# Gate and up projections of four SwiGLU layers as seven products of half width, two chunks at a time

## The chip, the cores and the metric

The kernel runs on one core of a Trainium2 chip. The metric is the device time of one execution in microseconds; for the kernel before it is the median of three runs. The engines of a core are TensorE (PE; PEld is its loading of stationary blocks), VectorE (DVE), ScalarE (ACT), GpSimd (POOL) and SyncE (SP, which here only issues transfers). Each executes its own instructions in order and waits on the others by semaphores.

## What is computed

A trunk of two decoder layers on 512 tokens of width 1024, in float32. Each layer is: half a SwiGLU feed-forward, a token mixer, half a SwiGLU feed-forward, a gated embedding. The mixer is a gated linear recurrence (HGRN) in the first layer and latent attention (MLA) in the second. The change touches the feed-forward layers:

```python
def _rmsnorm(x, g):
    y = x * lax.rsqrt(jnp.mean(x * x, axis=-1, keepdims=True) + EPS)
    return y * g

def _swiglu(h, w_in, w_out):            # w_in: 1024 x 5632, w_out: 2816 x 1024
    gate, up = jnp.split(h @ w_in, 2, axis=-1)
    return (jax.nn.silu(gate) * up) @ w_out

for li in range(2):
    x = x + 0.5 * _swiglu(_rmsnorm(x, g[0]), ffn_w_in[li, 0], ffn_w_out[li, 0])
    h = _rmsnorm(x, g[1])
    x = x + mixer(h)                    # HGRN for li = 0, MLA for li = 1
    x = x + 0.5 * _swiglu(_rmsnorm(x, g[2]), ffn_w_in[li, 1], ffn_w_out[li, 1])
    x = x + sigmoid(_rmsnorm(x, g[3]) @ ple_w_gate[li]) * (p[li] @ ple_w_in[li])
return _rmsnorm(x, final_norm)
```

## The kernel before

Features lie on the 128 partitions and the 512 tokens on the free axis, so x is eight tiles of 128x512. A float32 product is made of three matmuls: each operand is split into a rounded half `hi` and the rest `lo`, and `mm3` (L141) adds hi·hi, hi·lo and lo·hi in PSUM.

All weights lie in one stream in HBM, `wall`, in the order of their use, in tiles of eight blocks of 128x128 (512 KB). `block` (L129) hands out the blocks; at the start of a tile it calls `fetch` (L115): SP loads the tile into one of three `raw` buffers (L119), ACT casts it to one of three `whi` buffers (L125), DVE subtracts to one of three `wlo` buffers (L126). `chain` (L147) runs the three matmuls for every block of the contraction and leaves a PSUM bank.

`ffn` (L233) is called four times. It runs two halves of 11 chunks of 128 hidden features. A chunk takes one tile for its gate chain and one for its up chain, 24 matmuls of 128x512 each. `rb` is the reciprocal root mean square of each token, spread over the partitions; the operand `xg` (split x times gain) doesn't hold it, so both chains are multiplied by it afterwards: DVE times rb (L240), ACT silu (L241), POOL times rb (L242), DVE up times gate (L243), and a split (L157 on ACT, L158 on DVE). After the 11 chunks come eight output chains over the 11 hidden tiles, and DVE adds half of each to x (L249). In the second half `post(m)` prepares the next stage's operand for each x tile as it is done, and `beside` puts unrelated small work in (rotary tables, an embedding).

What sets the order: the program is written for one core, and a scheduler orders each engine's instructions, by the order of the code and by priorities (`soon` draws a fetch or an eviction ahead). Within an engine the order is then fixed. Slots come from rings: `slot` takes the next buffer of a tag (s, v, r, o, p, b), and an instruction that writes a slot waits for the last reader of its former content. PSUM has two rings of four banks, `mm` and `aux`.

In the trace the stages follow each other: start to 33 us, first FFN to 381, HGRN to about 663, second FFN to 1042, embedding and shared keys to 1150, third FFN to 1480, MLA to 1800, fourth FFN to 2150, the last embedding and norm to 2222.

Of the kernel before, what the change touches and what calls it, by code (L numbers as in the profile page):

```python
# [9 lines left out]
F32 = mybir.dt.float32  # L10
F32R = mybir.dt.float32r
I32 = mybir.dt.int32
AF = mybir.ActivationFunctionType
# [9 lines left out]
NF = DFF // P  # L23
NH = NF // 2
A_HEADS = 8
# [29 lines left out]
def kernel(  # L55
# [38 lines left out]

    BUFS = {"s": 38, "v": 9, "r": 14, "o": 8, "p": 6, "b": 4}
    FETCH_OFF = 200
# [17 lines left out]

    def fetch(pieces=1):  # L115
        i = stream["tiles"]
        stream["tiles"] += 1
        raw = wpool.tile([P, WB * P], F32, tag="raw", bufs=3, name=name("raw"))
        nc.sync.dma_start(raw, wall[i])  # L119
        hi = wpool.tile([P, WB * P], F32R, tag="whi", bufs=3, name=name("whi"))  # L120
        lo = wpool.tile([P, WB * P], F32R, tag="wlo", bufs=3, name=name("wlo"))
        n = WB * P // pieces
        for p in range(pieces):
            s = slice(p * n, (p + 1) * n)
            act.copy(hi[:, s], raw[:, s])  # L125
            dve.tensor_tensor(out=lo[:, s], in0=raw[:, s], in1=hi[:, s].bitcast(F32), op=ALU.subtract)  # L126
        stream["ready"].append((hi, lo))

# [103 lines left out]

    def ffn(xg, rb, post, beside=None, primed=()):  # L233
        primed = list(primed)
        for half in range(2):
            hidden = []
            for f in range(NH):
                pg, pu = (primed.pop(0) if primed else chain(xg) for _ in range(2))
                g = slot("g", F32, "r")
                dve.tensor_tensor(out=g, in0=pg, in1=rb, op=ALU.mult)  # L240
                act.activation(g, g, AF.Silu)  # L241
                pool.tensor_tensor(out=g, in0=g, in1=rb, op=ALU.mult)  # L242
                dve.tensor_tensor(out=g, in0=pu, in1=g, op=ALU.mult)  # L243
                hidden.append(split(g, None, "o" if f < 4 else "v" if f < 8 else "s"))
                if half == 1 and f == 5 and beside is not None:
                    beside()
# [433 lines left out]
    def shared(sh, sin, cos):  # L680
        st, lat, kr = sh.st, sh.lat, sh.kr
        tab = slot("tab")
        pool.tensor_scalar(out=tab[0:64, :], in0=cos[0:64, :], scalar1=1.0, scalar2=1.0, op0=ALU.mult, op1=ALU.mult)
        pool.tensor_scalar(
            out=tab[64:128, :], in0=sin[64:128, :], scalar1=cs[64:128, C_SIGN : C_SIGN + 1], scalar2=1.0,
            op0=ALU.mult, op1=ALU.mult,
        )
        kt = slot("kt")
        dve.tensor_tensor(out=kt, in0=kr, in1=tab, op=ALU.mult)
        pj = aux_bank()  # L690
        pe.matmul(pj, jmat, kt, start=True, stop=True)
        krope = split(pj)
        _, rc = rows(st)
        cn = []
        for m in range(2):
            c = slot("cn")
            dve.scalar_tensor_tensor(
                out=c, in0=lat[m], scalar=gain(V_LAT, m), in1=rc, op0=ALU.mult, op1=ALU.mult
            )
            cn.append(split(c))  # L700
        return cn, krope


    def mla(xg, stats, cn, krope, sin, cos, post):
# [13 lines left out]
        def rope(group):  # L718
            pa, pb = chain(cq), chain(cq)
            qa, qb, ta, tb = (slot("rt", F32, "p") for _ in range(4))  # L720
            act.copy(qa, pa)
# [3 lines left out]
            dve.tensor_tensor(out=ta, in0=ta, in1=tb, op=ALU.subtract)  # L725
            h1, l1 = split(ta, None, "b")
# [3 lines left out]
            h2, l2 = split(qb, None, "b")  # L730
            res = []
# [164 lines left out]

    ffn(first.xg[0], rb, n1, prepare, primed)
# [4 lines left out]
    ffn(n2.xg[0], rows(n2.stats)[1], n3, lambda: held.append(embed(0)))  # L902
    n4 = Next([gcol(1, 0)])
# [14 lines left out]
    n5 = Next([gcol(1, 1)])  # L918
    ffn(n4.xg[0], rb, n5)
    n6 = Next([gcol(1, 2)])  # L920
    mla(n5.xg[0], n5.stats, cn, krope, sin, cos, n6)
    n7 = Next([gcol(1, 3)])
    ffn(n6.xg[0], rows(n6.stats)[1], n7, lambda: held.append(embed(1)))
    last(n7.xg[0], held[1], rows(n7.stats)[1])
# [12 lines left out]
def _stream(i):  # L937
    out = []

    def ffn(l, n):  # L940
        wi = i["ffn_w_in"][l, n]
        wo = i["ffn_w_out"][l, n]
        for half in range(2):
            for f in range(half * NH, half * NH + NH):
                out.append(_blocks(wi[:, f * P : (f + 1) * P]))
                out.append(_blocks(wi[:, DFF + f * P : DFF + (f + 1) * P]))
            out.append(_blocks(wo[half * NH * P : (half + 1) * NH * P]))

# [137 lines left out]
```

## Time and profile before

| | us |
|---|---|
| median of 3 runs (2223.89 to 2224.09) | 2224.09 |
| the profiled execution | 2224.34 |
| its span in the profile | 2222.2 |
| PE busy | 2200.4 |
| DVE busy | 1158.4 |
| ACT busy | 774.4 |
| POOL busy | 423.3 |

The span runs from the first to the last instruction of the profiled execution; the rest of its time lies around it. A busy share is a mean over stages; the windows of a stage show which engine it waits for. In rows of the timeline the first number is the start, the second the duration; in grouped rows stand the count, the busy time, the mean of one in ns and the idle time before them with what ended it.

### The profile page before, as it was taken

The page shows a single profiled execution, that of the slowest core. Times are in us where ns is not written, and L with a number is a line of the kernel's source. Part 1 is how long each engine was busy: PE and PEld are TensorE (multiplying, and loading weights), DVE is VectorE, ACT ScalarE, POOL GpSimd, SP SyncE. Part 2 cuts the span into 40 slices and gives each one's busy share as a digit, 9 for nine tenths or more (in the row PEclk, how much of TensorE's full clock was granted, in tenths as well). Part 3 has the DMA queues.
Part 4 walks back from the last instruction along what each step waited for, and adds up shares of the span by engine and source line. Part 5 has one row for each costly group of instructions (what it writes and reads, how often), then busy time and mean ns, then how long its engine had stood idle before and what let it go on. Part 6 is the DMA issues. An engine that isn't in the chain of part 4 may idle for free.

```text
span 2222.2 us, 26413 instructions
## 1 busy us (share of the span) xinstructions
PE 2200.4 (99%) x10434; PEld 1845.4 (83%) x10434; DVE 1158.4 (52%) x1798; ACT 774.4 (35%) x1125; POOL 423.3 (19%) x441
## 2 busy tenths in 40 slices
PE   8999999999999999999999999999999999999998
PEld 6888888899888888888888888888888888888887
DVE  5333544778775433444654333457677764334445
ACT  4222333323333322334533222346444443223244
POOL 2100111454522100111121011112111121001111
PEclk9999999999999999999999999999999999999999
DMA  4332332222223233333232333323223122333332
GB/s 161 102 96 95 100 95 93 87 61 67 67 67 105 95 95 96 109 99 95 86 105 95 95 97 101 97 86 96 66 85 92 53 86 95 95 95 108 101 95 67
DMA packets 60523, 204.42 MB, mean 92 GB/s; under 512 B 7408, under 2 KB 9584, under 8 KB 60400
## 3 DMA queue, kind: packets, MB, share of 16 engines
q1 hardware_dynamic: 59536, 201.28, 28.9%
q8 instruction: 82, 1.34, 0.3%
q10 hardware_dynamic: 864, 1.46, 0.2%
q14 instruction: 41, 0.34, 0.0%
HBM read 196.42 MB, written 2.10 MB: 89 GB/s over the span
## 4 chain that ended last, share of the span: by engine, by line
PE 96%; DVE 2%; ACT 1%; issue 0%; DMA 0%; POOL 0%; SPq 0%; DVEq 0%; ACTq 0%
PE mm L142 29%; PE mm L143 29%; PE mm L144 29%; PE aux L396 1%; PE aux L143 1%; PE aux L144 1%; PE aux L142 1%; PE aux L800 1%; PE aux L774 0%; PE aux L775 0%; PE aux L205 0%; PE aux L213 0%; DVE wlo L126 0%; PE aux L196 0%; DVE lo L158 0%
## 5 line engine op out<-in xcount | busy, mean ns | idle before, releaser
L143 PE MATMUL mm<-lo,whi 128*128 128x512 f32 x2824 | 1103.1, 391 | 2.1 <-DVE lo L161 2.0
L142 PE MATMUL mm<-hi,whi 128*128 128x512 f32 x2824 | 1095.8, 391 | 8.8 <-ACT whi L125 6.4
L144 PE MATMUL mm<-hi,wlo 128*128 128x512 f32 x2824 | 1100.7, 390 | 0.0
L125 ACT CAST whi<-raw 128x1024 fp32r<-128x1024 f32 (+2 forms) x372 | 386.4, 1041 | 1096.6 <-PE mm L143 790.8
L142 PEld LDWEIGHTS mm<-hi,whi 128*128 128x128 f32 x2824 | 530.5, 188 | 118.0 <-ACT whi L125 6.4
L143 PEld LDWEIGHTS mm<-lo,whi 128*128 128x128 f32 x2824 | 530.9, 188 | 110.9 <-DVE lo L161 4.1
L144 PEld LDWEIGHTS mm<-hi,wlo 128*128 128x128 f32 x2824 | 530.8, 188 | 108.5 <-DVE wlo L126 0.7
L126 DVE TENSOR_TENSOR wlo<-raw,whi 128x1024 fp32r<-128x1024 f32 (+2 forms) x372 | 463.6, 1248 | 271.3 <-ACT whi L125 251.4
L242 POOL TENSOR_TENSOR g<-g,rb 128x512 f32<-128x512 f32 x88 | 152.3, 1733 | 984.0 <-ACT g L241 984.0
L243 DVE TENSOR_TENSOR g<-mm,g 128x512 f32<-128x512 f32 x88 | 60.8, 691 | 263.5 <-PE mm L144 255.0
L240 DVE TENSOR_TENSOR g<-mm,rb 128x512 f32<-128x512 f32 x88 | 60.4, 690 | 206.0 <-PE mm L144 206.0
L179 POOL TENSOR_TENSOR sq<-sq,sq 128x512 f32<-128x512 f32 x55 | 80.5, 1464 | 335.2 <-ACT sq L174 334.3
L249 DVE SCALAR_TENSOR_TENSOR x<-mm,x 128x512 f32<-128x512 f32 x64 | 44.2, 690 | 106.8 <-PE mm L144 105.6
L160 ACT ACTIVATE hi<-x,vc 128x512 fp32r<-128x512 f32 x72 | 51.4, 718 | 77.1 <-DVE x L249 57.3
L789 POOL TENSOR_SCALAR P<-P,t 128x128 f32<-128x128 f32 (+1 forms) x64 | 35.3, 551 | 220.3 <-DVE t L788 189.1
L161 DVE SCALAR_TENSOR_TENSOR lo<-x,vc,hi 128x512 fp32r<-128x512 f32 x72 | 63.0, 883 | 25.2 <-ACT hi L160 25.1
L158 DVE TENSOR_TENSOR lo<-g,hi 128x512 fp32r<-128x512 f32 x88 | 60.0, 684 | 0.9 <-ACT hi L157 0.7
L786 ACT ACTIVATE P<-P,t,t 128x128 f32<-128x128 f32 (+1 forms) x64 | 42.0, 656 | 47.0 <-DVE t L783 46.8
L157 ACT CAST hi<-g 128x512 fp32r<-128x512 f32 x88 | 54.5, 621 | 6.9 <-DVE g L243 6.9
L241 ACT ACTIVATE g<-g 128x512 f32<-128x512 f32 x88 | 55.0, 628 | 1.4 <-DVE g L240 1.2
L142 PE MATMUL mm<-whi,hi 128*128 128x256 f32 x192 | 55.2, 288 | 0.0
L143 PE MATMUL mm<-wlo,hi 128*128 128x256 f32 x192 | 55.0, 287 | 0.0
(199 smaller groups left out, 1576.0 us busy)
## 6 DMA issues: line engine op xcount, KB each, us to landing
raw<-in_wall SPq DMA_DIRECT2D x367, 512.0 KB, 3.5
x<-in_xT SPq DMA_DIRECT2D x8, 256.0 KB, 6.3
qr<-hi SPq DMA_DIRECT2D x32, 64.0 KB, 2.0
qr<-lo SPq DMA_DIRECT2D x32, 64.0 KB, 2.0
out_dram<-o SPq DMA_DIRECT2D x8, 256.0 KB, 2.5
p<-in_pT ACTq DMA_DIRECT2D x4, 256.0 KB, 2.7
cs<-in_cst SPq DMA_DIRECT2D x1, 385.0 KB, 7.4
pos<-in_pos ACTq DMA_DIRECT2D x1, 256.0 KB, 3.3
```

What stands on the lines that cost most here:

```text
L125: act.copy(hi[:, s], raw[:, s])
L126: dve.tensor_tensor(out=lo[:, s], in0=raw[:, s], in1=hi[:, s].bitcast(F32), op=ALU.subtract)
L142: pe.matmul(out, a[0], b[0], start=first, stop=False)
L143: pe.matmul(out, a[0], b[1], start=False, stop=False)
L144: pe.matmul(out, a[1], b[0], start=False, stop=last)
L158: dve.tensor_tensor(out=lo, in0=src, in1=hi.bitcast(F32), op=ALU.subtract)
L161: dve.scalar_tensor_tensor(out=lo, in0=src, scalar=scale, in1=hi.bitcast(F32), op0=ALU.mult, op1=ALU.subtract)
L179: eng.tensor_tensor(out=self.acc, in0=self.acc, in1=sq, op=ALU.add)
L240: dve.tensor_tensor(out=g, in0=pg, in1=rb, op=ALU.mult)
L241: act.activation(g, g, AF.Silu)
L242: pool.tensor_tensor(out=g, in0=g, in1=rb, op=ALU.mult)
L243: dve.tensor_tensor(out=g, in0=pu, in1=g, op=ALU.mult)
```

## The change

Each FFN has 22 chunks. Chunks 0 and 1 stay as they were, but for POOL's multiplication by rb. The other 20 are taken in pairs. For a pair, the weights are a 2x2 matrix of blocks, gate and up against the even and the odd blocks of the contraction (each of the four is one tile, with four blocks for either chunk); x is a 2x2 matrix too, even and odd blocks against the first and the second half of the tokens. `product` runs 24 matmuls of 128x256; seven products (Strassen's scheme in Winograd's form) replace what were eight.

`mixes` forms the four sums of x that the products need, once for each FFN, after chunk 0: POOL multiplies x by its gain, DVE forms sums and differences of half width, and they are split. `pair` forms the sums of weights: two by a transfer that adds to a buffer already loaded (L290, issued by POOL), two by DVE (L310, L330); seven weight tiles are split instead of four (L128, L129). Banks are reused between products, and evictions add parts together (L300, L308, L315, L327, L328, L341).

The second multiplication by rb moves behind the output chains: L371 multiplies the output bank by 0.5 and rb, and L372 adds it to x. There are three groups of output chains, over 8, 8 and 6 chunks, instead of two over 11. The number of raw buffers goes from 3 to 5, and the rings change: s 38 to 40, v 9 to 8, r 14 to 9, p 6 to 8, b 4 to 2. Some splits in the shared keys and in MLA change their ring. The order of the weight tiles in HBM follows.

```diff
-    BUFS = {"s": 38, "v": 9, "r": 14, "o": 8, "p": 6, "b": 4}
+    BUFS = {"s": 40, "v": 8, "r": 9, "o": 8, "p": 8, "b": 2}
...
+    def mixes(nx):
+        col, xg = nx.cols[0], nx.xg[0]
+        res = []
+        for i in range(KC // 2):
+            be, bo = slot("be", F32, "r"), slot("bo", F32, "r")
+            for b, m in ((be, 2 * i), (bo, 2 * i + 1)):
+                pool.tensor_scalar(out=b, in0=x[m], scalar1=gain(col, m), scalar2=1.0, op0=ALU.mult, op1=ALU.mult)
+            ta, tb = slot("ta", F32, "r"), slot("tb", F32, "r")
+            one, two = slice(0, HT), slice(HT, T)
+            dve.tensor_tensor(out=ta[:, one], in0=be[:, one], in1=be[:, two], op=ALU.subtract)
+            dve.tensor_tensor(out=ta[:, two], in0=bo[:, two], in1=be[:, two], op=ALU.subtract)
...
+            sa, sb = split(ta), split(tb)
...
+    def product(out, w, b, first):
+        for e in range(2):
+            for i in range(KC // 2):
+                s = slice((4 * e + i) * P, (4 * e + i + 1) * P)
+                o = out[:, e * HT : (e + 1) * HT]
+                for n, (u, v) in enumerate(((0, 0), (0, 1), (1, 0))):
+                    pe.matmul(
+                        o, w[u][:, s], b[i][v], start=first and e + i + n == 0, stop=False, skip_group_check=True
+                    )
+
+    def pair(b, rb):
...
+        def summed(i, j):
+            raw = raw_tile(n + i)
+            nc.gpsimd.dma_start(raw, wall[n + j], accum_op=ALU.add)
+            return raw
+
+        with soon(FETCH_OFF):
+            ra = raw_tile(n)
+            w = halves_of(ra)
+        bx = aux_bank()
+        product(bx, w, b[0], True)
+        e1 = mm_bank()
+        with soon(EV_OFF):
+            act.copy(e1, bx)
+        with soon(FETCH_OFF):
+            rs = summed(2, 3)
+            w = halves_of(rs)
+        bz = aux_bank()
+        product(bz, w, b[4], True)
+        s5 = slot("s5", F32, "r")
+        with soon(EV_OFF):
+            act.copy(s5, bz)
+        with soon(FETCH_OFF):
+            dve.tensor_tensor(out=ra, in0=rs, in1=ra, op=ALU.add)
+            w = halves_of(ra)
+        product(bx, w, b[5], False)
+        e2 = mm_bank()
+        with soon(EV_OFF):
+            dve.tensor_tensor(out=e2, in0=bx, in1=s5, op=ALU.add)
+        with soon(FETCH_OFF):
+            rc = raw_tile(n + 1)
+            w = halves_of(rc)
+        product(e1, w, b[1], False)
...
+        with soon(FETCH_OFF):
+            w = halves_of(summed(0, 2))
+        product(bx, w, b[6], False)
...
+        with soon(FETCH_OFF):
+            dve.tensor_tensor(out=rc, in0=ra, in1=rc, op=ALU.add)
+            w = halves_of(rc)
+        product(e2, w, b[2], False)
...
+        with soon(FETCH_OFF):
+            w = halves_of(raw_tile(n + 3))
+        product(e3, w, b[3], False)
...
             for m in range(KC):
                 po = chain(hidden)
-                dve.scalar_tensor_tensor(
-                    out=x[m], in0=po, scalar=0.5, in1=x[m], op0=ALU.mult, op1=ALU.add
-                )
-                if half == 1:
+                t = slot("t", F32, "r")
+                dve.scalar_tensor_tensor(out=t, in0=po, scalar=0.5, in1=rb, op0=ALU.mult, op1=ALU.mult)
+                dve.tensor_tensor(out=x[m], in0=t, in1=x[m], op=ALU.add)
```

Of the new order, three places. First DVE's rows of some two chunks in the middle of the first FFN, before the change (wlo: the lo half of a weight tile; lo: that of a hidden tile):

```order
L240 TENSOR_TENSOR g124_742<-mm116_680,rb54_280 128x512
L126 TENSOR_TENSOR wlo134_786<-raw132_783,whi133_785 128x1024
L243 TENSOR_TENSOR g124_742<-mm120_711,g124_742 128x512
L126 TENSOR_TENSOR wlo141_826<-raw139_823,whi140_825 128x1024
L158 TENSOR_TENSOR lo126_748<-g124_742,hi125_747 128x512
L240 TENSOR_TENSOR g135_813<-mm127_751,rb54_280 128x512
L126 TENSOR_TENSOR wlo145_857<-raw143_854,whi144_856 128x1024
L243 TENSOR_TENSOR g135_813<-mm131_782,g135_813 128x512
L126 TENSOR_TENSOR wlo152_897<-raw150_894,whi151_896 128x1024
L158 TENSOR_TENSOR lo137_819<-g135_813,hi136_818 128x512
```

and the rows of about one pair at the same place in the changed kernel (raw: a weight tile; mm and aux: PSUM banks; g: the gate's tile):

```order
L310 TENSOR_TENSOR raw154_866<-raw159_899,raw154_866 128x1024
L334 TENSOR_TENSOR g123_630<-mm136_727,rb54_280 128x2x256
L129 TENSOR_TENSOR wlo161_903<-raw159_899,whi160_902 128x1024
L341 SCALAR_TENSOR_TENSOR g123_630<-s5133_696,g123_630 128x2x256
L341 SCALAR_TENSOR_TENSOR g123_630<-mm143_791,g123_630 128x2x256
L129 TENSOR_TENSOR wlo165_935<-raw154_866,whi164_934 128x1024
L166 TENSOR_TENSOR lo150_858<-g123_630,hi149_857 128x512
L129 TENSOR_TENSOR wlo169_967<-raw167_964,whi168_966 128x1024
L166 TENSOR_TENSOR lo152_862<-g123_630,hi151_861 128x512
L330 TENSOR_TENSOR raw167_964<-raw154_866,raw167_964 128x1024
L129 TENSOR_TENSOR wlo172_999<-raw170_995,whi171_998 128x1024
L315 TENSOR_TENSOR mm166_962<-aux157_872,s5163_931 128x512
```

Seven weight halves and two sums of whole tiles now stand in a pair, with six evictions between them; the sum in the first of these buffers (L310) needs the tile that an adding transfer fills.

Second, DVE's rows at the start of the second FFN, before the change:

```order
L126 TENSOR_TENSOR wlo917_5580<-raw915_5577,whi916_5579 128x1024
L126 TENSOR_TENSOR wlo921_5611<-raw919_5608,whi920_5610 128x1024
L240 TENSOR_TENSOR g900_5496<-mm892_5434,rb891_5432 128x512
L240 TENSOR_TENSOR g911_5567<-mm903_5505,rb891_5432 128x512
L243 TENSOR_TENSOR g900_5496<-mm896_5465,g900_5496 128x512
L243 TENSOR_TENSOR g911_5567<-mm907_5536,g911_5567 128x512
L126 TENSOR_TENSOR wlo928_5651<-raw926_5648,whi927_5650 128x1024
L158 TENSOR_TENSOR lo902_5502<-g900_5496,hi901_5501 128x512
L158 TENSOR_TENSOR lo913_5573<-g911_5567,hi912_5572 128x512
```

and now, from the weight half of the first pair's first product (wlo1093) on; wlo1098 is that of its second:

```order
L129 TENSOR_TENSOR wlo1093_6714<-raw1091_6711,whi1092_6713 128x1024
L310 TENSOR_TENSOR raw1091_6711<-raw1096_6744,raw1091_6711 128x1024
L129 TENSOR_TENSOR wlo1098_6748<-raw1096_6744,whi1097_6747 128x1024
L357 TENSOR_TENSOR g1044_6560<-mm1036_6498,rb1035_6496 128x512
L252 TENSOR_TENSOR ta1049_6572<-be1047_6568 128x256
L253 TENSOR_TENSOR ta1049_6572<-bo1048_6569,be1047_6568 128x256
L254 SCALAR_TENSOR_TENSOR tb1050_6573<-ta1049_6572,bo1048_6569 128x256
L359 TENSOR_TENSOR g1044_6560<-mm1040_6529,g1044_6560 128x512
L257 SCALAR_TENSOR_TENSOR tb1050_6573<-tb1050_6573,bo1048_6569 128x256
L252 TENSOR_TENSOR ta1057_6590<-be1055_6586 128x256
L166 TENSOR_TENSOR lo1052_6579<-ta1049_6572,hi1051_6578 128x512
L253 TENSOR_TENSOR ta1057_6590<-bo1056_6587,be1055_6586 128x256
```

with the end of the same stretch, up to the eviction L315:

```order
L330 TENSOR_TENSOR raw1104_6809<-raw1091_6711,raw1104_6809 128x1024
L166 TENSOR_TENSOR lo1070_6619<-tb1066_6609,hi1069_6618 128x512
L257 SCALAR_TENSOR_TENSOR tb1074_6627<-tb1074_6627,bo1072_6623 128x256
L166 TENSOR_TENSOR lo1076_6633<-ta1073_6626,hi1075_6632 128x512
L321 TENSOR_TENSOR g1090_6710<-mm1095_6742,rb1035_6496 128x2x256
L129 TENSOR_TENSOR wlo1109_6844<-raw1107_6840,whi1108_6843 128x1024
L359 TENSOR_TENSOR g1087_6702<-mm1083_6671,g1087_6702 128x512
L166 TENSOR_TENSOR lo1078_6637<-tb1074_6627,hi1077_6636 128x512
L166 TENSOR_TENSOR lo1089_6707<-g1087_6702,hi1088_6706 128x512
L129 TENSOR_TENSOR wlo1112_6876<-raw1104_6809,whi1111_6875 128x1024
L315 TENSOR_TENSOR mm1103_6807<-aux1094_6717,s51100_6776 128x512
```

Between the weight half wlo1098 and L315 now stand 36 more rows, 16 of them the sums of x.

Third, TensorE's rows at that place, after the first product (whi1097, whi1101 and whi1105 are the weights of the second, third and fourth product):

```order
L274 MATMUL aux1099_6751<-hi1051_6578,whi1097_6747 128x256
L274 MATMUL aux1099_6751<-lo1052_6579,whi1097_6747 128x256
L274 MATMUL aux1099_6751<-hi1051_6578,wlo1098_6748 128x256
L274 MATMUL aux1099_6751<-hi1059_6596,whi1097_6747 128x256
L274 MATMUL aux1094_6717<-hi1053_6582,whi1101_6779 128x256
L274 MATMUL aux1094_6717<-lo1054_6583,whi1101_6779 128x256
L274 MATMUL aux1094_6717<-hi1053_6582,wlo1102_6780 128x256
L274 MATMUL aux1094_6717<-hi1061_6600,whi1101_6779 128x256
L274 MATMUL mm1095_6742<-hi994_6329,whi1105_6811 128x256
L274 MATMUL mm1095_6742<-lo995_6330,whi1105_6811 128x256
L274 MATMUL aux1099_6751<-lo1060_6597,whi1097_6747 128x256
L274 MATMUL aux1099_6751<-hi1059_6596,wlo1098_6748 128x256
```

Three products are taken in turns here as their parts of x come; and L315 stands ahead of whatever writes the bank aux1094 again for the fifth.

More of the change, by code (lines that the diff above doesn't have):

```diff
@@ L234, in ffn, with keep @@
+    def ffn(nx, rb, post, beside=None, primed=()):
         primed = list(primed)
-        for half in range(2):
+        xg, b = nx.xg[0], None
+        for lo, hi in GROUPS:
             hidden = []
[L237 to L246, printed above, removed]
+            def keep(h):
+                hidden.append(split(h, None, "o" if len(hidden) < 4 else "v"))
+            for f in range(lo, hi):
+                if f < PLAIN:
+                    pg, pu = (primed.pop(0) if primed else chain(xg) for _ in range(2))
+                    g = slot("g", F32, "r")
+                    dve.tensor_tensor(out=g, in0=pg, in1=rb, op=ALU.mult)
+                    act.activation(g, g, AF.Silu)
+                    dve.tensor_tensor(out=g, in0=pu, in1=g, op=ALU.mult)
+                    keep(g)
+                    if f == 0:
+                        b = mixes(nx)
+                elif f % 2 == 0:
+                    for h in pair(b, rb):
+                        keep(h)
+                    if f == 18 and beside is not None:
+                        beside()
@@ L719, in rope @@
             pa, pb = chain(cq), chain(cq)
-            qa, qb, ta, tb = (slot("rt", F32, "p") for _ in range(4))
+            qa, qb, ta, tb = (slot("rt") for _ in range(4))
             act.copy(qa, pa)
```

82 lines of the change are left out of this document (62 added, 20 removed).

## The prediction

> **What bounds the kernel now.** I read the table of engines, then the chain that ended last, then the windows of single stages, and last the rows of the operations that the change adds.
>
> ```profile
> PE 2200.4 (99%) x10434; PEld 1845.4 (83%) x10434; DVE 1158.4 (52%) x1798; ACT 774.4 (35%) x1125; POOL 423.3 (19%) x441
> PE 96%; DVE 2%; ACT 1%; issue 0%; DMA 0%; POOL 0%; SPq 0%; DVEq 0%; ACTq 0%
> 33.00:381.00 348.00, 348.00 (x1562) 289.13 (x1561) 147.32 (x172) 101.24 (x125) 46.53 (x29) 1.00 0.31 100
> 381.00:645.00 264.00, 264.00 (x1517) 233.27 (x1516) 199.76 (x437) 81.17 (x129) 126.57 (x207) 1.00 0.23 71
> 1480.00:1800.00 320.00, 315.55 (x1702) 271.05 (x1701) 231.09 (x510) 165.29 (x319) 59.27 (x80) 1.00 0.25 76
> 2150.00:2222.00 72.00, 63.35 (x313) 53.29 (x311) 37.08 (x58) 30.52 (x48) 9.57 (x9) 0.94 0.23 73
> ```
>
> TensorE is busy for 99% of the span and carries 96% of the chain. The window rows (start and end, length, busy time of PE, PEld, DVE, ACT and POOL, granted clock, DMA share) are the first FFN, HGRN, MLA and the end. In an FFN TensorE has no gap at all, while DVE is busy 147 of 348 us. So only fewer matmul nanoseconds help there, and DVE has room, unless work bunches up. A stage is then worth exactly the matmuls that it no longer has, plus the gaps that it gains.
>
> **Products.** A matmul's own duration overlaps the next; what counts is the distance of starts.
>
> ```profile
> 99.93 0.39 PE L142 MATMUL mm<-hi,whi 128*128 128x512 f32 x1
> ...
> 105.83 0.39 PE L144 MATMUL mm<-hi,wlo 128*128 128x512 f32 x1
> 384.98 0.28 PE L144 MATMUL mm<-whi,lo 128*128 128x256 f32 x1
> ...
> 390.37 0.28 PE L144 MATMUL mm<-whi,lo 128*128 128x256 f32 x1
> ```
>
> The first two rows lie 26 matmuls apart: 5.90 / 26 = 226.9 ns for 512 columns. The others lie 45 apart: 119.8 ns for 256, in HGRN, with a new stationary block for nearly every one. So half the width costs 53%, not 50%. Two chunks took 4 chains of 24: 96 x 226.9 = 21.78 us. Seven products of 24 take 168 x 119.8 = 20.13 us. That is 1.65 us a pair, times 40 pairs: **-66 us**. An eighth less arithmetic should give 12.5%; the narrower matmul leaves 7.6%.
>
> The Trainium skill, page "TensorE: Matmul & The Clock Gate", section "Back-to-back issue gap", gives N/2.4 + 2.5 ns for an isolated warm matmul. By it a pair would save 96 x 215.8 - 168 x 109.2 ns = 2.37 us, 95 us in all (an estimate from that page). The rows lie some 11 ns above the formula at both widths, so the trace disagrees.
>
> **Mixing.** Each FFN now forms, from x, eight POOL rows (L249 of the changed kernel), 16 DVE rows of half width and eight splits. Row by row:
>
> ```profile
> L126 DVE TENSOR_TENSOR wlo<-raw,whi 128x1024 fp32r<-128x1024 f32 x364 | 456.4, 1254 | 270.2 <-ACT whi L125 250.4 <-issue 6.2 <-PE aux L213 1.2
> L243 DVE TENSOR_TENSOR g<-mm,g 128x512 f32<-128x512 f32 x88 | 60.8, 691 | 263.5 <-PE mm L144 255.0 <-POOL g L242 8.5
> L158 DVE TENSOR_TENSOR lo<-g,hi 128x512 fp32r<-128x512 f32 x88 | 60.0, 684 | 0.9 <-ACT hi L157 0.7
> L382 DVE TENSOR_TENSOR qq<-qq,T 128x256 f32<-128x256 f32 x16 | 8.3, 521 | 0.0
> L611 DVE TENSOR_TENSOR o<-xf,aux 128x256 f32<-128x256 f32 x14 | 4.8, 411 | 0.7 <-PE aux L598 0.7
> L125 ACT CAST whi<-raw 128x1024 fp32r<-128x1024 f32 x364 | 382.8, 1052 | 1095.8 <-PE mm L143 790.8 <-issue 289.1 <-PE mm L144 6.6
> L335 POOL TENSOR_SCALAR k<-k,lbt 128x512 f32<-128x512 f32 x8 | 10.6, 1321 | 30.6 <-ACT k L330 30.6
> ```
>
> A half-width row lies between 0.411 and 0.521 us; I take 0.45. POOL's eight take 8 x 1.3 = 10.6 us, and start early, since x is done; POOL also loses the 88 multiplications by rb. It is DVE that is late. Its queue is in order, and in the second and fourth FFN it stands like this, counted from the start of chunk 0's gate chain (one chain = 24 x 226.9 = 5.44 us). There are three whi/wlo buffers, so the lo half of the first pair's second operand must wait until chunk 1's gate chain has freed one: 3 x 5.44 = 16.3, plus the cast 1.05 and its own 1.25: 18.6 us. Before the change such a wait was harmless, because little but evictions stood behind it. Now 36 rows stand between it and the eviction L315 that lets the fifth product write its bank; with L315 itself they are 16 half rows (7.2), 10 lo halves (6.84), 4 chunk evictions (2.76), four weight lo halves and the sum L330 (5 x 1.25 = 6.27), L321 and L315 (1.38): 24.5 us, so 43.1. TensorE is ready for the fifth product after four plain chains and four products: 4 x 5.44 + 0.65 (transposes) + 4 x 2.88 = 33.9. A stall of **9.2 us**, twice. In the third FFN the rows of shared() stand in the queue too, nine of them (6.2 us, less 1.5 of TensorE's own): **13.9**. In the first FFN:
>
> ```profile
> 28.84 3.50 DVE L126 TENSOR_TENSOR wlo<-raw,whi 128x1024 fp32r<-128x1024 f32 x3 [0.65 <-ACT whi L125]
> 35.35 1.05 ACT L125 CAST whi<-raw 128x1024 fp32r<-128x1024 f32 x1 [1.15 <-PE mm L143]
> 671.68 2.31 DVE L126 TENSOR_TENSOR wlo<-raw,whi 128x1024 fp32r<-128x1024 f32 x1
> 682.27 1.22 DVE L126 TENSOR_TENSOR wlo<-raw,whi 128x1024 fp32r<-128x1024 f32 x1
> ```
>
> DVE can begin at 28.84; seven weight lo halves, two sums, and the same small rows come to 29.5 us, so about 58.3, while TensorE has ended the primed chains at about 35.2 and four products at 46.7: **12 us**. Together 9.2 + 9.2 + 13.9 + 12 = **+44 us**. The last two rows show a DVE row at 2.31 instead of 1.22 us while POOL works beside it; POOL's eight rows beside the mixing may so add 1.1 us to one row in each FFN, up to 10.6 us in each if every POOL microsecond is lost to DVE. I take **+5** in all, nearer the first. The bounds of this part: 20 us (half of the stall, if half rows go at 0.41 and the scheduled order lets products 2 to 4 spread) to 44 + 42.
>
> **A steady pair.** DVE has seven weight lo halves and two sums (9 x 1.254 = 11.3), six evictions and products (4.1) and two lo halves (1.4): 16.8 of 20.1 us, where it was 9.1 of 21.8. It fits, and every product's operands come in time by these rows, except through the adding DMAs, which no row of before shows.
>
> ```profile
> raw<-in_wall SPq DMA_DIRECT2D x367, 512.0 KB, 3.5
> cs<-in_cst SPq DMA_DIRECT2D x1, 385.0 KB, 7.4
> q1 hardware_dynamic: 59536, 201.28, 28.9%
> L189 POOL TENSOR_TENSOR t<-t,mhalf 128x4 f32<-128x4 f32 x18 | 21.3, 1183 | 118.3 <-DVE t L186 118.2
> ```
>
> A tile lands 3.5 us after issue, and the 16 engines need 0.289 x 2222.2 us for 201.28 MB, 1.67 us for one tile. The loop: L330 frees a raw buffer; the next pair's tile 0 and, behind it on SP's queue, its tile 2 land 5.2 us later; the adding DMA takes A; then DVE does L310, L334, a weight half, two L341, a weight half, a lo half, a weight half, a lo half and L330 (9.7 us in this order). One turn is 14.9 + A; it costs nothing up to A = 5.2. Beyond, the products' operands come A - 5.2 later with each turn, and TensorE waits once the lag is over the 2.7 us by which they are early. Each group starts anew: 2, 3 and 2 turns. A is at least 3.5, a load's time, and at most 8.6 (the slowest load of a kind, 7.4, and 1.18, taken for POOL's issue from its row of four columns). I take 6.3 = 3.5 + 1.67 (the old sums read back too) + 1.18: lag 1.1, 2.1, 3.2, so 0.5 us an FFN, **+2**. At 8.6 it is 4.1 + 7.5 + 4.1 = 15.7 an FFN, +63.
>
> **Rings and ends.** The ring r goes from 14 to 9, b from 4 to 2, in HGRN too, where DVE is busy 200 and POOL 127 of 264 us. Bounds: nothing, if TensorE stays covered as in the row above, and 8 heads x (1.321 + 1.008) = 18.6 us if POOL's two rows of each head's gate had to wait for a slot (second price from the next row). I take **+3**, nearest to nothing since TensorE has no gap there.
>
> ```profile
> L332 POOL TENSOR_SCALAR f<-f,lbt 128x512 f32<-128x512 f32 x8 | 8.1, 1008 | 0.0
> ```
>
> The second x row of an output chain (0.69) hides under the next chain (8 blocks, 5.44 us) but for each FFN's last; with the rotary work now beside the last group: **+2**.
>
> **Sum.** 2224.34 (profiled execution) - 66 + 44 + 5 + 2 + 3 + 2 = 2214.3; the median stands 0.25 lower: **2214 us**, -0.45%. A measurement of this kernel tells about 0.2% from no change: 2219.6 to 2228.5 counts as the same.
>
> **Rivals.**
> - *Mixing is hidden better*: DVE's half rows take 0.41, or the lo half that waits comes free earlier. The stall halves to 20 us: 2190. For it: 201 us of DVE's time in an FFN are idle. Against it: 37 rows in order. 0.13.
> - *The adding DMA is late* (slower): at A = 8 the turn is 22.9 us; the lags 2.8, 5.5, 8.3 less 2.7 give 2.8 + 5.6 + 2.8 = 11.3 us an FFN, 45 in all: 2257. It decides from A = 6.8, where the sum crosses 2228.5. For it: a 385 KB load took 7.4. Against it: 367 loads with a median of 3.5. 0.20.
> - *Rings*: +18.6 in place of 3: 2230. 0.10.
> - *TensorE's clock falls in the new gaps*: the last window row has 8.65 us idle and clock 0.94, 0.06 x 72 = 4.3 us lost. Four stalls at 4.3 each: 2231. Against it: while TensorE waits for DVE, slower products before the wait cost nothing. 0.07.
> - *The narrow matmuls issue faster in the products* than in HGRN, at exactly half of 226.9, 113.4 ns: 6.4 ns x 6720 = 43 us, 2171. Against it: 45 even steps at 119.8. 0.03.
>
> On the fourth: the same page of the Trainium skill, section "Why this matters for your kernels", says that one idle stretch above about 3 us takes the clock back to half, so each of the four stalls would be followed by slow matmuls. The end's 0.94 agrees with it; how long the slow time lasts after one such gap, no row shows.
>
> **How the numbers follow.** Forecast 0.47, its own range 2203 to 2228 (of it faster 0.35, same 0.12); with the rivals, faster 0.51, same 0.18 (some of the ring and clock cases end there), slower 0.31. The range goes from the better-hidden mixing, 2186, to the late DMA, 2258.
>
> **What would show it.** Products 119.8 ns apart inside a pair, and pairs 20.1 us apart; four TensorE gaps of 9 to 14 us ended by DVE L315 or L166 at the starts of the FFNs; DVE busy about 17 us in each pair. It is wrong if TensorE waits inside steady pairs on L310 or L129 behind the adding DMA (A over 5.2), if gaps appear in HGRN, or if the clock falls below 1.00 after the stalls.

## The result, and the profile after

| | before | changed |
|---|---|---|
| median, us | 2224.05 (2223.86 to 2224.47, 9 runs) | 2236.71 (2227.93 to 2240.90, 9 runs) |
| the profiled execution, us | 2224.34 | 2234.61 |
| its span, us | 2222.2 | 2232.8 |
| ratio to before, 95% interval | | 1.0052, [1.0040, 1.0065] |

The change costs 12.7 us, 0.6%; the forecast was 2214 us, 10 less than before. The runs now spread over 13 us, where they lay within 0.6.

The table of engines, the queues, the chain that ended last and the transfers of the changed kernel, from its page:

```profile
PE 2167.8 (97%) x13314; PEld 1948.5 (87%) x13314; DVE 1578.2 (71%) x2302; ACT 964.5 (43%) x1357; POOL 386.4 (17%) x465
...
q0 software_dynamic: 11520, 41.95, 10.7%
...
PE 67%; DVE 7%; DMA 5%; issue 2%; ACT 2%; POOL 0%; DVEq 0%; POOLq 0%; ACTq 0%; SPq 0%
...
raw<-in_wall SPq DMA_DIRECT2D x407, 512.0 KB, 3.6
raw<-in_wall POOLq DMA_DIRECT2D x80, 512.0 KB, 6.8
```

TensorE is busy for 33 us less than before and yet the span is 11 us longer: what was won is lost in waits and at a lower clock, and the chain, which was TensorE's at 96%, now runs over DVE and transfers as well. The median adding transfer takes 6.8 us from issue to landing, the median load 3.6.

Six stretches of the changed kernel in the windows view (start and end, length, busy time of PE, PEld, DVE, ACT and POOL, clock, DMA share): the first pair of the first FFN, the pair behind it, a pair in the middle, the last pair of the first FFN, the first pair of the second FFN, and the pair behind that. Then the first pairs of the third and fourth FFN.

```profile
35.27:67.70 32.43, 25.93 (x169) 24.11 (x168) 26.87 (x40) 14.53 (x21) 8.78 (x7) 0.84 0.47 116
67.70:87.86 20.16, 20.16 (x170) 20.16 (x169) 13.48 (x16) 9.47 (x13) 0.87 (x1) 1.00 0.55 157
194.51:215.46 20.95, 20.41 (x170) 20.21 (x169) 15.66 (x18) 10.65 (x14) 1.74 (x2) 1.00 0.66 172
322.05:351.90 29.85, 24.14 (x175) 23.55 (x174) 21.89 (x28) 13.63 (x17) 0.00 (x0) 0.89 0.40 124
713.41:741.26 27.85, 22.83 (x170) 21.82 (x169) 23.90 (x35) 14.05 (x19) 7.80 (x5) 0.94 0.41 108
741.26:761.42 20.16, 20.16 (x171) 20.16 (x170) 13.74 (x16) 9.69 (x13) 1.73 (x2) 1.00 0.64 171
...
1149.62:1175.52 25.90, 23.84 (x170) 22.69 (x169) 20.94 (x30) 14.72 (x22) 2.69 (x4) 0.91 0.36 102
1833.21:1861.71 28.50, 24.29 (x170) 23.14 (x169) 24.03 (x36) 14.04 (x19) 8.06 (x5) 0.88 0.41 107
```

An undisturbed pair takes 20.16 us, with TensorE never idle: the 20.13 of the prediction. The four first pairs take 12.3, 7.7, 5.7 and 8.3 us more, 34 together. Part of it is a lower clock and not waiting: (1 - clock) x length, 5.2 + 1.7 + 2.3 + 3.4 = 12.6 us, is its upper bound, since some of the slow time falls into waits; by the distances of the matmuls it is some 11 us, and 23 are waits. The last pair of the first FFN loses about 9. The pair in the middle loses 0.8; such losses of 0.3 to 1.7 come in 17 of the 28 pairs that follow a pair, 14 us together by the distances of their first matmuls.

What TensorE waited for in the changed kernel (engine, line and releaser; us in total, times, longest):

```profile
PE aux L274 <- ACT mm L300: 12.1, 19, 1.6
PE aux L274 <- DVE mm L315: 10.3, 5, 5.6
PE aux L221 <- POOL t L197: 8.2, 3, 6.8
PE mm L150 <- ACT whi L128: 6.3, 1, 6.3
PE mm L274 <- DVE wlo L129: 5.5, 4, 2.3
```

The fourth row is the start, which was there before. The first one was not in the prediction: ACT's copy L300 of the first product's bank, 19 times.

### The profile page after: what moved, and what is told of

Read it like the earlier page. It is cut to its first block, busy times and chain, and to the rows that moved or that the text cites. A ratio compares the mean times of both kernels' runs of the same rounds, so it can differ in the third digit from the quotient of the medians.

```text
span 2232.8 us, 33475 instructions
## 1 busy us (share of the span) xinstructions
PE 2167.8 (97%) x13314; PEld 1948.5 (87%) x13314; DVE 1578.2 (71%) x2302; ACT 964.5 (43%) x1357; POOL 386.4 (17%) x465
## 4 chain that ended last, share of the span: by engine, by line
PE 67%; DVE 7%; DMA 5%; issue 2%; ACT 2%; POOL 0%; DVEq 0%; POOLq 0%; ACTq 0%; SPq 0%
PE mm L150 14%; PE mm L151 14%; PE mm L152 14%; PE aux L274 9%; PE mm L274 7%; DMA raw<-in_wall 5%; DVE wlo L129 3%; PE aux L517 1%; PE aux L151 1%; PE aux L152 1%; PE aux L150 1%; ACT whi L128 1%; PE aux L921 1%; DVE lo L166 1%; DVE g L341 1%
## 5 line engine op out<-in xcount | busy, mean ns | idle before, releaser
L128 ACT CAST whi<-raw 128x1024 fp32r<-128x1024 f32 (+1 forms) x492 | 510.6, 1039 | 878.9 <-PE mm L151 453.2
L129 DVE TENSOR_TENSOR wlo<-raw,whi 128x1024 fp32r<-128x1024 f32 (+1 forms) x492 | 608.0, 1237 | 167.1 <-ACT whi L128 157.9
L150 PE MATMUL mm<-hi,whi 128*128 128x512 f32 x1544 | 598.3, 393 | 11.3 <-ACT whi L128 6.3
L151 PE MATMUL mm<-lo,whi 128*128 128x512 f32 x1544 | 606.2, 393 | 2.1 <-DVE lo L169 2.0
L152 PE MATMUL mm<-hi,wlo 128*128 128x512 f32 x1544 | 603.1, 392 | 0.0
L274 PE MATMUL aux<-hi,whi 128*128 128x256 f32 x1280 | 367.8, 288 | 23.1 <-ACT mm L300 12.1
L274 PE MATMUL aux<-lo,whi 128*128 128x256 f32 x1280 | 365.7, 286 | 3.6 <-DVE lo L166 3.5
L274 PE MATMUL aux<-hi,wlo 128*128 128x256 f32 x1280 | 365.0, 285 | 0.3 <-DVE wlo L129 0.2
L274 PE MATMUL mm<-hi,wlo 128*128 128x256 f32 x960 | 275.0, 286 | 5.5 <-DVE wlo L129 5.5
L274 PE MATMUL mm<-hi,whi 128*128 128x256 f32 x960 | 274.3, 286 | 0.5 <-ACT mm L300 0.5
L274 PEld LDWEIGHTS aux<-hi,whi 128*128 128x128 f32 x1280 | 248.1, 194 | 29.6 <-ACT mm L300 16.3
L290 POOL DMA_DIRECT2D raw<-in_wall x80 | 70.4, 880 | 1054.6 <-DMA raw<-in_wall 522.6
L371 DVE SCALAR_TENSOR_TENSOR t<-mm,rb 128x512 f32<-128x512 f32 x96 | 66.0, 688 | 186.7 <-PE mm L152 186.7
```

The lines of the kernel that those rows point to most:

```text
L150: pe.matmul(out, a[0], b[0], start=first, stop=False)
L151: pe.matmul(out, a[0], b[1], start=False, stop=False)
L152: pe.matmul(out, a[1], b[0], start=False, stop=last)
L274: pe.matmul(o, w[u][:, s], b[i][v], start=first and e + i + n == 0, stop=False, skip_group_check=True)
L290: nc.gpsimd.dma_start(raw, wall[n + j], accum_op=ALU.add)
L371: dve.scalar_tensor_tensor(out=t, in0=po, scalar=0.5, in1=rb, op0=ALU.mult, op1=ALU.mult)
```

## The experiments

**Without pairs.**

```diff
-PLAIN = 2
+PLAIN = NF
...
-                    if f == 0:
-                        b = mixes(nx)
+                    if f == 18 and beside is not None:
+                        beside()
```

> All 22 chunks of each FFN plain: no products, no sums of x or of weights; groups of 8, 8 and 6, the rings, five raw buffers and rb behind the output chains stay as changed. Theory A (the excess of the changed kernel lies in the pairs: first pairs of the FFNs, adding transfers, rotary rows beside a pair): 2224 to 2229 us, with TensorE gaps outside the FFNs of under 10 us. Rival B (the smaller rings cost HGRN and MLA most of it): 2240 us or more.

Measured: 2232.19 us (2231.67 to 2232.97), between the two. So 8.1 us of the loss have nothing to do with the products. The new gaps lie at the end of HGRN: the chain of L197 and L221 and a split in front of the output projection, 3.9 us by the distances of matmuls, where the kernel before had none.

**The ring r, with all chunks plain.**

```diff
-    BUFS = {"s": 40, "v": 8, "r": 9, "o": 8, "p": 8, "b": 2}
+    BUFS = {"s": 40, "v": 8, "r": 13, "o": 8, "p": 8, "b": 2}
...
-        raw = wpool.tile([P, WB * P], F32, tag="raw", bufs=5, name=name("raw"))
+        raw = wpool.tile([P, WB * P], F32, tag="raw", bufs=3, name=name("raw"))
```

> The run with all chunks plain again, but three raw buffers in place of five and the space given to the ring r: 13 slots in place of 9. Theory A (the ring r is what costs the 8 us there; the new gap of 3.9 us at the end of HGRN waits for its slots): 2225 us, and that gap is gone. Rival B (it is the work behind the output chains, the groups, or the other rings): 2230 to 2233 us.

Measured: 2227.57 us (2225.81 to 2229.66, ten runs), 4.6 less. TensorE's waits of the run with 9 slots, then of this one:

```profile
PE aux L221 <- POOL t L197: 1.5, 2, 1.1
PE mm L150 <- ACT hi L165: 2.0, 2, 1.3
```

```profile
PE mm L150 <- ACT hi L165: 0.7, 1, 0.7
```

The wait on L197 is gone, and with it the gap at the end of HGRN. Rings are worth 4.6 of the 8.1 us. Two numbers changed at once, so r and raw aren't told apart here; the other 3.5 us (groups, rb behind the output chains, the other rings) weren't split further.

**Without the sums of x.**

```diff
-            be, bo = slot("be", F32, "r"), slot("bo", F32, "r")
...
-            sa, sb = split(ta), split(tb)
...
-                for part, t in ((e, one), (o, one), (o, two), (sb, two), (sa, one), (sb, one), (sa, two))
+                for part, t in ((e, one), (o, one), (o, two), (e, two), (e, one), (e, two), (o, one))
```

> The sums of x are left out (plain halves of x times gain stand in their place), so POOL's eight rows, 16 DVE rows and eight splits of each FFN are gone; everything else stays. Theory A: the four first pairs lose their stalls and the slow clock behind them (32.4, 27.9, 25.9 and 28.5 us in place of 20.2, and the 6.8 us in front of the third): about 43 us less, 2194 us. Rival B (the first pairs wait for their weights, not for x): less than 15 us of it goes, 2222 us or more.

Measured: 2203.05 us (2195.42 to 2207.24), 33.7 less: the first pairs' 34 us. Three of them then take 20.15 us; that of the third FFN takes 22.1, without a wait inside it, as its first matmuls still run at the clock of 0.50 that follows the wait in front of it. That wait stayed:

```profile
PE aux L221 <- POOL t L197: 7.0, 3, 5.5
```

So that wait, 6.8 us in the changed kernel, isn't made by the sums of x. The root of the shared keys' norm goes from TensorE (L213) over DVE (L215, L194) and POOL (L197) back to TensorE (L221), with L221 next in TensorE's order; nothing of the products, which stand behind it, fills the time. With all chunks plain the wait isn't there: a plain chain stands in its place.

**Four plain chunks.**

```diff
-PLAIN = 2
+PLAIN = 4
```

> Four plain chunks ahead of the pairs in each FFN in place of two (nine pairs in place of ten); the sums of x still come after the first. Theory A: the first pairs' stalls (34 us in the pairs) hide behind two more plain chunks, for 4 x 1.64 = 6.6 us of products: about 2209 us, and 2200 if the stall ahead of the third FFN goes too. Rival B (DVE has so much to do that the stall only moves back): 2235 to 2245 us.

Measured: 2195.62 us (2195.12 to 2198.86), 41.1 less though 6.6 us of products were given back (and eight of the 80 adding transfers with them). All four first pairs take 20.2 us, not counting the plain chain that runs between the products of the third FFN's, and the wait in front of the third FFN falls to about 3 us in two pieces (other rows now stand between L213 and L221). The sums of x aren't too much work; they come in a place with too little of TensorE's own beside them.

**The sums of x ahead of chunk 0.**

```diff
-        xg, b = nx.xg[0], None
+        xg, b = nx.xg[0], mixes(nx)
...
-                    if f == 0:
-                        b = mixes(nx)
```

> The changed kernel with mixes called ahead of chunk 0 instead of after it; by that the sums of x stand on DVE ahead of the weight half that waits for a free buffer (third chain's end), not behind it. Nothing is left out. Theory A (the stall is the order in DVE's queue, not its load): the first pairs of the second and fourth FFN fall from 27.9 and 28.5 us to about 20.2, that of the first loses about half of its 12; 2212 us. Rival B (DVE is simply full there): first pairs within 2 us of before this turn, 2230 us or more.

Measured: 2238.78 us (2235.20 to 2242.44): nothing won. The mechanism was right and the result wrong. The first pairs of the second and fourth FFN do fall to 20.1 and 20.2 us, but the sums now stand ahead of the rows of the norm (L215, L194), and TensorE waits there:

```profile
PE aux L221 <- POOL t L197: 19.3, 6, 6.4
```

19.3 us in place of 8.2. Turning the queue round hands the wait to the next one in it; of the two turns, only the one with more cover, in the run before, won time.

**Without the adding transfers.**

```diff
         def summed(i, j):
             raw = raw_tile(n + i)
-            nc.gpsimd.dma_start(raw, wall[n + j], accum_op=ALU.add)
             return raw
```

> The 80 adding transfers are left out (the buffer holds one tile in place of the sum of two); everything else stays. Theory A: the waits of 0.5 to 1.2 us in pairs that follow a pair go, about 16 us: 2220 us, and the runs come within 1 us of each other instead of 13. Rival B (the five loads of a pair on SP's queue set those waits, not the adding): no change, 2233 to 2239 us, though with less spread.

Measured: 2217.28 us (2216.53 to 2218.83): 19.4 less, and a spread of 2.3 us in place of 13. In its trace every pair between the first and last of an FFN is 20.16 us long (20.6 where other work stands in it). The adding transfers cost 19 us by the medians, not 2, and most of the spread comes with them. Between the two traces the difference is 15.8: the 14 us of the pairs that follow a pair, and 1.6 in the last pair of the first FFN.

**The summed tile asked for first.**

```diff
         with soon(FETCH_OFF):
+            rs = summed(2, 3)
             ra = raw_tile(n)
             w = halves_of(ra)
...
         with soon(FETCH_OFF):
-            rs = summed(2, 3)
             w = halves_of(rs)
```

> The changed kernel with one order turned: each pair asks for the buffer of its first summed tile, and its adding transfer, ahead of the first product's tile, so that neither stands on SP's queue behind the load that waits for L330. Theory A (the adding transfer's 6.8 us behind that wait are what steady pairs wait for): the waits in pairs that follow a pair shrink, 2220 to 2224 us. Rival B (the five buffers turn too fast for it, or the second summed tile is the late one): 2233 to 2239 us.

Measured: 2225.33 us (2224.16 to 2230.17, ten runs), 11.4 less, with all the arithmetic in it. In its trace all but three of the pairs that follow a pair (one of the three is the last of the first FFN) have no wait, while the first pairs take up to 1.4 us longer than in the changed kernel. Where did the waits sit? The changed kernel's rows of DVE, ACT and TensorE, some left out, in a pair that follows a pair, from the timeline (start, duration, engine, operation, and in brackets the idle time before it and what ended it):

```profile
173.06 1.23 DVE L310 TENSOR_TENSOR raw<-raw,raw 128x1024 f32<-128x1024 f32 x1 [3.04 <-DMA raw<-in_wall]
173.06 1.05 ACT L128 CAST whi<-raw 128x1024 fp32r<-128x1024 f32 x1 [4.42 <-DMA raw<-in_wall]
...
175.88 1.04 ACT L128 CAST whi<-raw 128x1024 fp32r<-128x1024 f32 x1
...
177.92 1.05 ACT L128 CAST whi<-raw 128x1024 fp32r<-128x1024 f32 x1
178.87 0.61 ACT L165 CAST hi<-g 128x512 fp32r<-128x512 f32 x1
179.39 0.57 ACT L300 COPY mm<-aux 128x512 f32<-128x512 f32 x1
180.02 0.39 PE L274 MATMUL aux<-hi,whi 128*128 128x256 f32 x1 [1.05 <-ACT mm L300]
```

ACT stands idle for 4.4 us until the sum has landed, and everything behind that cast in its queue is late: a silu, two casts, two splits, and then L300, which must empty the first product's bank before the third product may write to it. TensorE, which had its weights, waits 1.05 us for a copy. ACT's waits for transfers ahead of its casts in the changed kernel, and with the order turned; last TensorE's waits for the copy (L301 there) with the order turned, which in the changed kernel were 12.1 us in 19 waits:

```profile
ACT whi L128 <- DMA raw<-in_wall: 78.7, 25, 4.4
...
ACT whi L128 <- DMA raw<-in_wall: 0.4, 1, 0.4
PE aux L274 <- ACT mm L301: 1.0, 1, 1.0
```

The turned order brings the transfer forward as a whole; a run that moves only the copy ahead of the cast in ACT's queue wasn't made.

One turn of the loop in the changed kernel, from the end of L330 in the pair at 172.79 to its end in the pair at 194.51:

```profile
180.75 1.22 DVE L330 TENSOR_TENSOR raw<-raw,raw 128x1024 f32<-128x1024 f32 x1
186.12 0.87 POOL L290 DMA_DIRECT2D raw<-in_wall  x1 [11.91 <-DMA raw<-in_wall]
194.01 1.23 DVE L310 TENSOR_TENSOR raw<-raw,raw 128x1024 f32<-128x1024 f32 x1 [2.27 <-DMA raw<-in_wall]
201.70 1.22 DVE L330 TENSOR_TENSOR raw<-raw,raw 128x1024 f32<-128x1024 f32 x1
```

The turn takes 20.95 us, and so does the pair: 4.2 to the issue of the adding transfer, 7.8 until it has landed, 9.0 for DVE's rows. The 28 first adding transfers of pairs that follow a pair take 7.9 us in the median (5.7 to 9.8), the other 52 take 5.8. How late L310 may be is seen in three such pairs, whose first matmuls start at 741.25, 845.84 and 1175.53 us:

```profile
738.44 1.21 DVE L310 TENSOR_TENSOR raw<-raw,raw 128x1024 f32<-128x1024 f32 x1
844.53 1.23 DVE L310 TENSOR_TENSOR raw<-raw,raw 128x1024 f32<-128x1024 f32 x1 [1.46 <-DMA raw<-in_wall]
1174.55 1.22 DVE L310 TENSOR_TENSOR raw<-raw,raw 128x1024 f32<-128x1024 f32 x1 [1.80 <-DMA raw<-in_wall]
```

In the first, L310 didn't wait for the sum and starts 2.8 us ahead of its pair. Started 1.3 us ahead (the second) it costs nothing yet, started 1.0 us ahead (the third) it costs 0.3: there are about 1.5 us to lose, and then L300 is late.

**The rotary rows beside the output chains.**

```diff
-                    if f == 18 and beside is not None:
-                        beside()
...
+                if hi == 16 and m == 0 and beside is not None:
+                    beside()
```

> The changed kernel with the work that stands beside the chunks (rotary tables in the first FFN, the embedding's halves in two others) moved from the pair of chunks 18 and 19 to the output chains of the second group. Theory A (DVE has 3.3 us free in a pair, and the rotary rows delay L315 by 5.6 us there): the wait of 5.6 us and the slow clock behind it go, 2228 us. Rival B (they delay the x updates or the next pair as much): no change, 2233 to 2239 us.

Measured: 2226.17 us (2219.51 to 2233.97, ten runs), 10.5 less, with the wide spread of the adding transfers. The last pair of the first FFN falls from 29.85 to 22.0 us; the wait for L315 there, the longest in the table of the changed kernel (5.6), is gone.

**Gaps made on purpose in the kernel before.**

```diff
+            for _ in range(1 + {8: 8, 16: 10, 38: 12, 46: 15}.get(i, 0)):
+                dve.tensor_tensor(out=lo[:, s], in0=raw[:, s], in1=hi[:, s].bitcast(F32), op=ALU.subtract)
```

> The kernel before, with the weight lo half of four tiles of the first FFN computed 9, 11, 13 and 16 times instead of once, so that TensorE waits for DVE at four places of a stage that had no gap: about 1.4, 3.9, 6.4 and 10.1 us by 1.25 us a row and a lead of 8.6 us. Theory A (a gap over some 2 us takes the clock down for several us after it, 2 to 3 us lost each time): the gaps and 6 to 9 us more, about 2253 us. Rival B (only the gaps cost): 2246 us, granted clock 1.00 behind them.

Measured: 2238.95 us (2238.21 to 2239.05), 14.8 more than before. Only the last of the four made a gap; the others were hidden, so the lead was more than the 8.6 us that was counted on. TensorE's rows round it, and the windows ahead of it, of the first 3.4 us of the gap and the rest of it, right behind it, and further on:

```profile
274.64 0.39 PE L145 MATMUL mm<-hi,wlo 128*128 128x512 f32 x1
286.47 0.79 PE L145 MATMUL mm<-hi,wlo 128*128 128x512 f32 x1 [11.44 <-DVE wlo L127]
287.06 0.63 PE L143 MATMUL mm<-hi,whi 128*128 128x512 f32 x1
287.49 0.63 PE L144 MATMUL mm<-lo,whi 128*128 128x512 f32 x1
```

```profile
250.00:274.00 24.00, 24.00 (x108) 19.87 (x107) 20.13 (x27) 5.37 (x6) 1.80 (x1) 1.00 0.26 77
275.10:278.50 3.40, 0.00 (x0) 0.00 (x0) 3.40 (x5) 0.79 (x1) 0.00 (x0) 1.00 0.31 120
278.60:286.40 7.80, 0.00 (x0) 0.00 (x0) 7.80 (x10) 0.63 (x1) 0.00 (x0) 0.50 0.24 67
286.47:292.15 5.68, 5.68 (x13) 4.46 (x14) 2.17 (x4) 1.82 (x3) 2.51 (x2) 0.50 0.28 92
292.00:300.00 8.00, 8.00 (x36) 6.57 (x36) 3.24 (x5) 2.40 (x4) 0.00 (x0) 0.99 0.23 66
```

The gap is 11.4 us, the loss 14.8: the clock falls to 0.50 some 3.5 us into the gap and stays there for 5.7 us behind it, in which matmuls start 0.43 us apart instead of 0.227, and that costs some 2.8 us more. Short waits take the clock down as well, as the changed kernel's first pair shows. The windows ahead of its first fall of the clock, and behind it:

```profile
38.33:41.74 3.41, 1.86 (x7) 0.97 (x6) 3.41 (x6) 2.54 (x4) 2.73 (x2) 1.00 0.06 24
41.75:48.57 6.82, 4.95 (x23) 4.96 (x24) 6.82 (x13) 1.21 (x3) 1.85 (x1) 0.50 0.00 0
```

TensorE was busy for 1.86 of 3.41 us there, idle in pieces of at most 0.5 us, and the clock is 0.50 for the next 6.8 us.

**Together.** Two plain chunks with mixes ahead, the sum first and the rotary rows moved; then four plain chunks with mixes in its place and the other two; then that with four raw buffers and 11 slots of r. The edit of the second:

```diff
-PLAIN = 2
+PLAIN = 4
...
+            rs = summed(2, 3)
             ra = raw_tile(n)
...
+                if hi == 16 and m == 0 and beside is not None:
+                    beside()
```

> Three turns of order together, with two plain chunks: mixes ahead of chunk 0, the summed tile's buffer asked for first, the rotary rows beside the output chains. Nothing is left out. Theory A (the parts add): that with mixes ahead, less 11 for the adding transfers and 9 for the rotary rows: about 2192 us. Rival B (what one frees another takes): over 2210 us.

Measured: 2212.21 us (2209.82 to 2215.34): the parts don't add up, as the rival had it. The waits of TensorE on L197 that mixes ahead brings are still 16.3 us.

> Four plain chunks, the summed tile's buffer asked for first, the rotary rows beside the output chains; mixes after chunk 0 as changed. Nothing is left out. Theory A (the parts add): 2195.6 less 8.5 for the rotary rows and some 9 for the transfers: about 2178 us. Rival B: over 2190 us.

Measured: 2180.76 us (2179.77 to 2181.85), near the 2178 of the sum; ratio to before 0.9802, [0.9786, 0.9819].

> As the run with four plain chunks and all turns of order, with four raw buffers instead of five and the space given to the ring r: 11 slots instead of 9. Nothing is left out. Theory A (the ring r makes the gap at the end of HGRN, and a pair can live on four buffers, as one of its tiles waits anyway): the gap there (3.9 us and the slow clock behind it) goes, 2175 us. Rival B (the pairs' loads then come late, as a pair uses five tiles): waits in steady pairs, 2190 us or more.

Measured: 2201.71 us (2199.60 to 2208.36). Pairs wait again (0.4 to 1.7 us in eleven of them, mostly on the copy of the first bank) and MLA gets new small waits: the fifth buffer is needed more than the two slots of r. At the end of HGRN one wait of 2.6 us on L197 stays.

Of the second of these, the engines, the chain, and TensorE's longest waits:

```profile
PE 2149.3 (99%) x13026; PEld 1925.0 (88%) x13026; DVE 1554.4 (71%) x2274; ACT 952.6 (44%) x1337; POOL 369.5 (17%) x457
...
PE 94%; DVE 3%; issue 1%; ACT 1%; DMA 1%; POOL 0%; SPq 0%; DVEq 0%; POOLq 0%; ACTq 0%
```

```profile
PE mm L150 <- ACT whi L128: 6.5, 1, 6.5
PE mm L150 <- DVE g L357: 3.4, 3, 1.4
```

The chain is TensorE's again, at 94%, and the longest wait is that of the start.

## Why the prediction was wrong

The sum had six terms. Beside each, what the runs put in its place:

| term | predicted | measured | from |
|---|---|---|---|
| products | -66 | -65 | 40 x (21.78 - 20.16) |
| first pairs (mixing, POOL beside it) | +49 | +34 (23 of waits, 11 of the lower clock), and 6.8 ahead of the third FFN | pair lengths; 33.7 by the run without the sums |
| adding transfers | +2 | +19.4 (14 in the pairs of the trace) | the run without them |
| rings | +3 | +4.6 | ring r at 13, raw at 3 |
| ends, rotary rows beside | +2 | +8 to 10 | pair length; the run with them moved |
| groups, rb behind the chains, the rest | (in the ends) | 3.5 | all chunks plain, less the rings |

The right column adds up to about 12, the change measured to 12.7; the parts overlap, as each was taken away by itself, and the medians of runs with adding transfers are uncertain by a few us, so that the sum comes so close is partly luck.

- **The step that failed** is the slack in the loop of the adding transfer: "TensorE waits once the lag is over the 2.7 us by which they are early", which made +2. The 2.7 us were counted to the products' weights; but the summed tile's cast stands on ACT, in order, ahead of the copy L300, and by the rows above L310 can be only some 1.5 us late before TensorE waits for that copy. With 1.5 in place of 2.7 the prediction's own lags (1.1, 2.1, 3.2) give 0.6 + 1.7 + 0.6 = 2.9 us an FFN, 12 in all; the pairs of the trace lose 14. With the measured 19.4 in its place the sum would have been 2231, on the measured side of no change.
- **The turn of that loop** was forecast at 21.2 us and is 21.0, but by two errors that cancel: A was taken at 6.3 where the transfers in the loop take 7.9, and the rest at 14.9 where it takes 13.2. That is luck. The slower rival named this effect, and A came near its 8; yet it put the cost at 45 us, as it had the same 14.9. Nor does it decide from A = 6.8: by the loop's own formula the sum is 2225 there and crosses 2228.5 at about 6.9.
- **The rotary rows** were costed at next to nothing, although the steady pair's own line said that only 3.3 us of DVE were free in it. In the last pair of the first FFN DVE is busy 21.9 us, and L315 waits behind the rows. That the work now stood in a place with 3.3 us of free DVE, where two chunks of before had 21.8 - 9.1 = 12.7, was not followed.
- **The clock** was given 0.07 as a rival. In the first pairs it costs some 11 us, where the rival had 17. Its rows stand above: 0.50 from 3.5 us into a gap of 11.4 us on. The Trainium skill, page "TensorE: Matmul & The Clock Gate", section "Why this matters for your kernels", says that an idle stretch of over some 3 us brings the clock back to half; that gap agrees. But the first pair's clock fell when no wait had yet lasted longer than 0.5 us, and at the end of HGRN it falls to 0.50 at 669.8 us after waits of at most 1.1 us. The 0.94 at the end of the kernel before, which the prediction read as agreeing, is of this kind too: its clock falls at 2213.5 us, after one wait of 1.05 us. So staying under that length doesn't keep the clock up here.
- **Mixing** came out smaller than forecast all the same, because the stall itself was put too high: four first pairs lose 23 us to waiting where 44 were forecast, in several waits of at most 2.6 us each and not in one gap of 9 to 14. In the third FFN 13.9 was the estimate, and 5.7 came in the pair and 6.8 ahead of it. The queue behind the waiting weight half, the reason given, holds for the second and fourth FFN (with it turned, their first pairs fall to 20.1 and 20.2); that too little of TensorE's own stands beside the rows fits the four plain chunks.
- **Products**: right, to 1 us. The narrow matmuls start 119.8 ns apart in the products as in HGRN, so the rival at 113.4 ns isn't borne out, and the 109.2 ns by the Trainium skill's formula for an isolated matmul, which the prediction gives, aren't reached in this stream.
- **Direction**: two errors of opposite sign (the stall put too high, the clock left out of the sum) made up for part of one another; the transfers and the rotary rows, 24 us too low together, turned the sign.

What stays open: what the time of an adding transfer is made of, why the first of a pair that follows a pair takes 7.9 us and the others 5.8, and why the runs spread so with them; whether it is r or the number of raw buffers that makes the gap at the end of HGRN; how much idle time within a few us halves the clock.

## What to carry to other kernels

When an operation gets a long or uncertain wait, don't ask only when its result is needed: ask what stands behind it on its engine. Here a cast that waited for a transfer held up an eviction that had nothing to do with it, and asking for the slow transfer first was worth 11 us by the medians (8.7 between the traces) without touching any arithmetic. And a burst of set-up work needs cover on the bound engine: two more chunks an FFN done the old way cost 6.6 us of products and won 41 net.

## What was not expected of the hardware

An adding transfer of 512 KB takes 6.8 us in the median (5.7 with the other order), a load of the same size 3.6; and where pairs wait for them the runs spread by 4 to 14 us, against 1.3 to 3.9 in the three kernels without them and 2.1 where the waits are hidden. A gap of 11.4 us is followed by 5.7 us at clock 0.50, then by full speed at once; and waits of at most 0.5 us, close together, bring the same clock. POOL's product by a column takes 0.68 us at its shortest in the trace, and 1.0 and 1.8 on the mean of its two rows. Most of the long ones stand beside a busy DVE, but so do four of 0.69 us at 1136 us; what makes the difference isn't shown:

```profile
L249 POOL TENSOR_SCALAR bo<-x,vc 128x512 f32<-128x512 f32 x16 | 29.2, 1828 | 5.9 <-DVE tb L257 4.5 <-DVE ta L253 0.7 <-DVE lo L166 0.6
L249 POOL TENSOR_SCALAR be<-x,vc 128x512 f32<-128x512 f32 x16 | 16.4, 1027 | 8.7 <-DVE ta L253 4.1 <-PE aux L213 4.0 <-POOL bo L249 0.4
```
